# Norms between products in a two-layer trunk: one written order for all engines

## The chip, the cores and the metric

The kernel runs on one core of a Trainium2 chip. The metric is the device time in microseconds (us) from launch to the last store, as the median of several executions. One more execution was recorded by the hardware profiler; its trace gives start and length of each instruction on TensorE (PE, with its weight loads as PEld), VectorE (DVE), ScalarE (ACT), GpSimd (POOL) and SyncE (SP, which here only issues DMAs).

## The reference

Two layers over 512 tokens of 1024 features in float32. Each layer is a mixer and a gated MLP, and each of the two has a norm before and a norm after it:

```
x = x + rms_norm(mix, norm_gains[layer, 1])      # post-norm of the mixer
u = rms_norm(x, norm_gains[layer, 2])            # pre-norm of the MLP
ff = conv_ffn(u, ...)                            # 1024 -> 2 x 2816, conv of width 3, silu(gate) * val, -> 1024
x = x + rms_norm(ff, norm_gains[layer, 3])       # post-norm of the MLP
```

`rms_norm` divides each token's row by the root of its mean square (plus 1e-6) and multiplies by a gain per feature. The mixer of layer 0 runs four mLSTM heads and four gated DeltaNet heads, that of layer 1 eight HGRN2 heads; both end in a product with an output matrix of 1024 x 1024.

## The kernel before

**Precision.** Every large product is made of three matmuls on operands split in a high and a low part: high x high, high x low, low x high (`mm3`, lines 211 to 214). A weight piece of 128 x 1024 is loaded into a buffer `raw` (three of them), ACT copies the upper part (`whi`, line 230), and DVE or POOL subtracts it for the lower part (`wlo`, through the helper on line 101). `whi` and `wlo` have six places each, `PIECES`.

**Layout.** Tokens form four tiles of 128. The stream `xs` is kept with tokens in partitions. The normalised input `u` of a product is kept turned, features in partitions, as upper and lower parts `uh` and `ul` of eight blocks (k) by 512 tokens.

**A norm.** Of a post-norm, `postnorm_half` squares one half row of a product's PSUM bank on ACT (`token_square`, line 184, with the sum read out behind it) and multiplies the bank by the gain on DVE. `token_rsqrt` makes the root for 128 tokens: a sum on DVE (`tr_v`), Sqrt on ACT (`tk_y`), then a reciprocal and one Newton step on DVE (`tk_q`, `tk_r`). `postnorm_tile` adds bank times root to x, in two halves. The pre-norm `prenorm_tile` squares the halves of x, takes the root, scales to `un` (line 104), turns it by four PE transposes per half (`ut`, line 240), and ACT and DVE take the upper (line 235) and lower part into `uh` and `ul`.

**The three places.** `mix_out` multiplies the mixer's output with the output matrix: for column half n = 0, then n = 1, for all four token tiles t, 24 matmuls each into a bank `mo`; behind each (1, t) follows the post-norm of tile t, and behind some of them a pre-norm of one or two tiles, by the list `TAILS`. The MLP then starts with five pieces of the up-projection in two passes, first 256 tokens and last 256 (`EARLY`), so that PE can begin before the last tiles are normalised. The down-projection of the MLP keeps eight banks `dn` open; the last four of its 22 blocks are done bank by bank, and the norms follow in the same way, in layer 0 with the pre-norm of layer 1, whose first products are the value columns (`pt`), and in layer 1 with the stores.

**What sets the order.** Instructions written plainly are ordered per engine by a planner, by their place in the program and its own costs and readiness; a tile of a pool waits until its place is free. `then(f, ...)` ties an instruction behind the last one that was so tied on the same engine, so that these keep their written order on it; `now(f, ...)` issues plainly. A `tc.issue_after(ins)` block puts what it holds behind one instruction. All loads go through SP's queue in its order.

Of the kernel before, what the change touches and what calls it, by code (L numbers as in the profile page):

```python
# [18 lines left out]
P = 128  # L19
# [12 lines left out]
TAILS = ((0,), (1,), (), (2, 3))  # L32
# [3 lines left out]
def kernel(  # L36
# [24 lines left out]
    stop: int = 4,  # L61
# [65 lines left out]


# [10 lines left out]
    def load_x(xt, t, eng=nc.sync):  # L139
        eng.dma_start(out=xt[:, t, :], in_=x[0, t * P : (t + 1) * P, :])  # L140
# [42 lines left out]
    def now(f, **kw):  # L183
        f(**kw)

# [25 lines left out]
    def mm3(ps, lh, ll, rh, rl, start, stop):  # L211
        T.matmul(ps, lhsT=lh, rhs=rh, start=start, stop=False)  # L212
        T.matmul(ps, lhsT=lh, rhs=rl, start=False, stop=False)  # L213
        T.matmul(ps, lhsT=ll, rhs=rh, start=False, stop=stop)  # L214

    def load_w(src):
# [4 lines left out]
        nc.sync.dma_start(out=rv, in_=src)  # L221
        return rv
# [28 lines left out]
    def put_half(u, t, h, src):  # L251

        ps = mxt("ut")
        transpose4(ps, src, range(4))
        sl = (slice(None), slice(4 * h, 4 * h + 4), slice(t * P, (t + 1) * P))
        split_ps(u[0][sl], u[1][sl], v4(ps))

# [5 lines left out]
    def prenorm_tile(xt, t, g, u):  # L263
        ss = col(2, "ss")
        for h, hs in enumerate(halves):
            token_square(xt[:, hs], ss[:, h : h + 1])
        r = token_rsqrt(ss)
        for h, hs in enumerate(halves):
            un = half_t("un")
            stt(un, xt[:, hs], r, g[:, hs], ALU.mult, ALU.mult)  # L270
            put_half(u, t, h, un)

    def postnorm_half(ps, h, g, ss):

        token_square(ps, ss[:, h : h + 1])
        tt(V, ps, ps, g[:, halves[h]], ALU.mult)

    def postnorm_tile(xt, banks, ss):
        r = token_rsqrt(ss)
        for hs, ps in zip(halves, banks):  # L280
            stt(xt[:, hs], ps, r, xt[:, hs], ALU.mult, ALU.add)
# [55 lines left out]
    EARLY = ((0, 256), (256, 512))  # L337


    def ffn(layer, cw, cb, xs, tail):  # L340

        w_up, w_down = ffn_w_up[layer], ffn_w_down[layer]
        with tc.tile_pool(name=f"ffn{layer}", bufs=1) as fp:
            def t2(name, dt=F32, bufs=2, tag=None):
# [4 lines left out]
            yield lambda t: prenorm_tile(xs[t], t, gpre, u)  # L349
            gpost = gain(layer, 3)  # L350
            h0 = big["B"].tile([P, KD, S], F32, tag="h", name="h0")
            h2 = fp.tile([P, NF - 2 * KD, S], F32, tag="h2", name="h2")
            hT = [h0[:, f, :] for f in range(KD)] + [eighth(f, "h1") for f in range(KD)]
            hT += [h2[:, f, :] for f in range(NF - 2 * KD)]
            wc = [w_up[:, f * P : (f + 1) * P] for f in range(2 * NF)]
            early = feature_blocks(
                [piece(wc[i], V) for i in (0, NF, 1, NF + 1, 2)], u, EARLY, [bank(g, "pf") for g in ("pj", "pj", "sc", "po", "sc")]
            )
            for f in range(NF):
                pg = early.pop(0) if early else feature_block(wc[f], u)  # L360
# [4 lines left out]
                pv = early.pop(0) if early else feature_block(wc[NF + f], u)  # L365
# [4 lines left out]
            banks = [[bank(g, "dn") for g in tg] for tg in tags]  # L370
            dv = w_down.rearrange("(k p) c -> p k c", p=P)
            hs = {}
            last = 4

            def step(k, t, n):
# [3 lines left out]
                    banks[t][n], hi[:, tsl], lo[:, tsl], w[0][:, 0, halves[n]], w[1][:, 0, halves[n]], k == 0, k == NF - 1  # L379
                )  # L380

            for k in range(NF):
# [6 lines left out]
                if k < NF - last:  # L389
# [3 lines left out]
            for t in range(NT):  # L393
                ss = col(2, "ss2")
                for n in range(2):
                    for k in range(NF - last, NF):
                        step(k, t, n)
                    postnorm_half(banks[t][n], n, gpost, ss)
# [896 lines left out]
    for layer in range(2):  # L1295
# [31 lines left out]
        for _ in it:  # L1327
            pass
# [60 lines left out]
```

## Time and profile before

| | |
|---|---|
| median of 3 executions | 1344.22 us (1343.63 to 1344.73) |
| the profiled execution: time, and span of its instructions | 1344.86 us, 1343.1 us |
| PE busy | 1321.3 us, 98% of the span |
| DVE, ACT, POOL busy | 665.1, 613.5, 363.7 us |
| products of the up-projection and the like (`pf`), matmuls | 1168 on each of the lines 212, 213, 214 |
| granted TensorE clock, mean | 0.999 |

A row of the timeline holds the start, the length, engine, line, operation, the tile written and those read, the shape and the number of instructions merged, and in brackets the engine's idle time before it with what ended it. A row of a group holds, after the count, the busy time, the mean length in ns and the idle time before. Matmuls overlap, so their distance is read from start to start.

### The profile page before, as it was taken

The page shows a single profiled execution, that of the slowest core. Times are in us where ns is not written, and L with a number is a line of the kernel's source. Part 1 is how long each engine was busy: PE and PEld are TensorE (multiplying, and loading weights), DVE is VectorE, ACT ScalarE, POOL GpSimd, SP SyncE. Part 2 cuts the span into 40 slices and gives each one's busy share as a digit, 9 for nine tenths or more (in the row PEclk, how much of TensorE's full clock was granted, in tenths as well). Part 3 has the DMA queues.
Part 4 walks back from the last instruction along what each step waited for, and adds up shares of the span by engine and source line. Part 5 has one row for each costly group of instructions (what it writes and reads, how often), then busy time and mean ns, then how long its engine had stood idle before and what let it go on. Part 6 is the DMA issues. An engine that isn't in the chain of part 4 may idle for free.

```text
span 1343.1 us, 20271 instructions
## 1 busy us (share of the span) xinstructions
PE 1321.3 (98%) x8029; PEld 1096.8 (82%) x8029; DVE 665.1 (50%) x1321; ACT 613.5 (46%) x1158; POOL 363.7 (27%) x195
## 2 busy tenths in 40 slices
PE   8999999999999999999999999999999999999997
PEld 8787887888988888888878878877798888888886
DVE  6863774457543333311276784786756333332114
ACT  6754663545443333322356554564644333333222
POOL 1000000000665555544200000000036555554440
PEclk9999999999999999999999999999999999999999
DMA  6521131143333333222234123221323333322211
GB/s 176 163 64 37 48 95 50 43 157 99 95 110 94 94 101 103 95 95 94 94 94 113 64 61 94 69 74 32 106 83 111 98 104 97 95 94 94 97 61 63
DMA packets 165564, 121.25 MB, mean 90 GB/s; under 512 B 9246, under 2 KB 151006, under 8 KB 165470
## 3 DMA queue, kind: packets, MB, share of 16 engines
q1 hardware_dynamic: 165470, 119.96, 29.1%
q8 instruction: 63, 1.03, 0.3%
q14 instruction: 31, 0.25, 0.1%
HBM read 117.85 MB, written 2.10 MB: 89 GB/s over the span
## 4 chain that ended last, share of the span: by engine, by line
PE 76%; DVE 6%; ACT 1%; issue 1%; DVEq 0%; ACTq 0%
PE pf L212 15%; PE pf L213 15%; PE pf L214 15%; PE dn L212 6%; PE dn L213 6%; PE dn L214 6%; PE mo L212 2%; PE mo L214 1%; DVE wlo L101 1%; PE mo L213 1%; PE lev L1135 1%; DVE xt L104 1%; PE pt L214 1%; PE pt L213 1%; PE pt L212 1%; DVE un L104 1%
## 5 line engine op out<-in xcount | busy, mean ns | idle before, releaser
L101 POOL TENSOR_TENSOR wlo<-raw,whi 128x1024 fp32r<-128x1024 f32 x122 | 294.1, 2411 | 628.2 <-ACT whi L230 333.4
L212 PE MATMUL pf<-uh,whi 128*128 128x512 f32 (+1 forms) x1168 | 442.0, 379 | 0.0
L213 PE MATMUL pf<-ul,whi 128*128 128x512 f32 (+1 forms) x1168 | 441.5, 378 | 0.4 <-DVE ul L101 0.4
L214 PE MATMUL pf<-uh,wlo 128*128 128x512 f32 (+1 forms) x1168 | 440.7, 377 | 0.0
L230 ACT CAST whi<-raw 128x1024 fp32r<-128x1024 f32 x206 | 215.9, 1050 | 226.0 <-PE pf L213 204.7
L104 DVE SCALAR_TENSOR_TENSOR acc<-pf,fcw,acc 128x511 f32<-128x511 f32 (+1 forms) x176 | 131.4, 749 | 279.8 <-ACT acc L332 276.9
L212 PEld LDWEIGHTS pf<-uh,whi 128*128 128x128 f32 x1168 | 219.8, 188 | 40.0 <-ACT uh L235 0.5
L213 PEld LDWEIGHTS pf<-ul,whi 128*128 128x128 f32 x1168 | 220.0, 188 | 38.9 <-DVE ul L101 0.9
L214 PEld LDWEIGHTS pf<-uh,wlo 128*128 128x128 f32 x1168 | 220.0, 188 | 38.2
L212 PE MATMUL dn<-whi,hh 128*128 128x512 f32 x352 | 137.2, 390 | 0.0
L214 PE MATMUL dn<-whi,hl 128*128 128x512 f32 x352 | 137.0, 389 | 0.0
L213 PE MATMUL dn<-wlo,hh 128*128 128x512 f32 x352 | 137.0, 389 | 0.0
L101 DVE TENSOR_TENSOR wlo<-raw,whi 128x1024 fp32r<-128x1024 f32 x84 | 105.4, 1257 | 60.2 <-ACT whi L230 56.5
L101 DVE TENSOR_TENSOR hl<-h,hh 128x512 fp32r<-128x512 f32 x44 | 31.6, 717 | 160.4 <-ACT hh L386 160.3
L386 ACT CAST hh<-h 128x512 fp32r<-128x512 f32 x44 | 27.4, 623 | 152.3 <-PE dn L213 131.5
L212 PEld LDWEIGHTS dn<-whi,hh 128*128 128x128 f32 x352 | 66.1, 188 | 14.2 <-issue 0.5
L213 PEld LDWEIGHTS dn<-wlo,hh 128*128 128x128 f32 x352 | 66.1, 188 | 13.7
L214 PEld LDWEIGHTS dn<-whi,hl 128*128 128x128 f32 x352 | 66.1, 188 | 13.7
L753 POOL TENSOR_SCALAR_AFFINE_SELECT dec<-dec 128x512 f32<-128x512 f32 x8 | 7.3, 909 | 243.9 <-DVE dec L101 178.7
L332 ACT ACTIVATE acc<-pf,fcb,fcw 128x512 f32<-128x512 f32 x88 | 68.1, 774 | 8.2 <-POOL sg L101 5.7
L101 POOL TENSOR_TENSOR sg<-sg,acc 128x512 f32<-128x512 f32 x44 | 57.9, 1315 | 31.0 <-ACT sg L363 31.0
L363 ACT ACTIVATE sg<-acc 128x512 f32<-128x512 f32 x44 | 27.8, 632 | 67.0 <-DVE acc L104 67.0
(344 smaller groups left out, 1601.1 us busy)
## 6 DMA issues: line engine op xcount, KB each, us to landing
raw<-in_ffn_w_up_dram SPq DMA_DIRECT2D x88, 512.0 KB, 3.8
raw<-in_ffn_w_down_dram SPq DMA_DIRECT2D x44, 512.0 KB, 3.2
raw<-in_c_w_in_dram SPq DMA_DIRECT2D x32, 512.0 KB, 4.0
raw<-in_ab_w_in_dram SPq DMA_DIRECT2D x26, 512.0 KB, 3.7
gain<-in_norm_gains_dram SPq DMA_DIRECT2D x8, 512.0 KB, 5.2
raw<-in_ab_w_out_dram SPq DMA_DIRECT2D x8, 512.0 KB, 3.9
raw<-in_c_w_out_dram SPq DMA_DIRECT2D x8, 512.0 KB, 4.0
x<-in_x_dram SPq DMA_DIRECT2D x4, 512.0 KB, 5.9
```

The source lines that it names most:

```text
L101: return eng.tensor_tensor(out=o, in0=a, in1=b, op=op)
L104: return V.scalar_tensor_tensor(out=o, in0=a, scalar=s, in1=b, op0=op0, op1=op1, **kw)
L212: T.matmul(ps, lhsT=lh, rhs=rh, start=start, stop=False)
L213: T.matmul(ps, lhsT=lh, rhs=rl, start=False, stop=False)
L214: T.matmul(ps, lhsT=ll, rhs=rh, start=False, stop=stop)
L230: A.copy(out=hv, in_=rv)
L332: A.activation(out=acc, in_=ps, func=AF.Identity, scale=taps[:, K - 1 : K], bias=bias)
L363: A.activation(out=sg, in_=ag, func=AF.Sigmoid)
L386: A.copy(out=hi, in_=hT[k])
L753: G.affine_select(out=v4(d), in_=v4(d), pattern=[[0, NT], [1, P]], compare_op=ALU.is_ge, fill=-BIG, base=0, channel_multiplier=-1,)
L1135: T.matmul(pl4[i * 64 : (i + 1) * 64, c], lhsT=kr[:, c * P + i * 64 : c * P + (i + 1) * 64], rhs=qf[:, :, at : at + 32], start=True, stop= ...
```

## The change

`TAILS`, `prenorm_tile`, `postnorm_half` and `postnorm_tile` go. A class `Norms` holds the same steps as single functions, each issued through `then`; `root` issues the sum and the Sqrt at once and returns the rest, for the gain product to be put between. Three functions write out the order in which all engines go through the three kinds of norm:

- `mix_out` (both layers): the products of tiles 0 to 2 of half 0, then (1,0), (1,1), (1,2), (0,3), (1,3), then three early pieces. The second two weight pieces of half 1 are split into the places of `hh` and `hl`, two up pieces ahead of the norms into `w2` and `acc`, a third between them. x of tiles 2 and 3 is loaded behind the first two up pieces.
- `into_next` (from layer 0 to 1): the four pieces of value weights are split first, two into `w2` and `acc`; the four value products take the place of the first `token_blocks` of the mixer.
- `last_norm` (end): the order of before, with the first two steps of the root ahead of the gain product.

Three MLP pieces instead of five are done in halves; the other two are split behind the norms. In layer 1's mixer the three pieces of a head are fetched and split together at its start.

```
+    class Norms:
+        def root(self, t, second=False):
+            steps = []
+            self.roots[t] = token_rsqrt(self.ss[t][second], lambda f, **kw: steps.append((f, kw)))
+            for f, kw in steps[:2]:
+                then(f, **kw)
+            return lambda: [then(f, **kw) for f, kw in steps[2:]]
...
+    def mix_out(w_dram, order, yhi, ylo, gpost, xs, fetch, gpre, u, wc, t2, w2):
...
+                rv = load_w(wv[:, 2 * q : 2 * q + 2, halves[n]])
+                if n and i > 1:
+                    late.append((q, rv))
+                    continue
+                hi, lo = split_w(rv, V)
...
+        def products(n, t, ins=(), do=then):
+            b = banks[n, t] = bank((("pj", "pj", "pj", "pj"), ("sc", "sc", "po", "sc"))[n][t], f"mo{t}")
+            sl = slice(t * P, (t + 1) * P)
+            for i, k in enumerate(order8):
+                for f in dict(ins).get(i, ()):
+                    f()
+                mm3(b, yhi[:, k, sl], ylo[k][:, sl], *ws[n, k], i == 0, i == KD - 1, do)
...
+        for t in range(2):
+            fetch(t)
+        for t in range(3):
+            products(0, t, do=now)
+            nm.squares(0, t, now)
+            nm.gains(0, t, now)
+        for q, rv in late:
+            late_split(q, rv)
+        raws = [raw(i) for i in EARLY[:2]]
+        for t in (2, 3):
+            fetch(t, then)
+        split(raws[:1], spare[:1], spare[1:2])
...
+        products(1, 0)
+        nm.squares(1, 0)
+        rest = nm.root(0)
+        nm.gains(1, 0)
+        rest()
+        nm.residual(0, 0)
+        nm.squares2(0, 0)
...
+        rest = nm.root(2)
+        products(0, 3, ((5, [nm.turned(1, 0)]), (6, [nm.turned(1, 1)])))
+        r_ = raw(EARLY[2])
...
+        products(1, 3)
+        take(lambda k: hi2[:, k, :], lambda k: lo2[:, k, :], "sc")
+        early(0, 0, ((4, [nm.turned(2, 0)]), (7, [nm.turned(2, 1)])))
+        nm.squares(1, 3)
+        rest = nm.root(3)
+        nm.gains(1, 3)
+        nm.upper(2, 0)
+        rest()
+        nm.upper(2, 1)
+        nm.residual(3, 0)
+        nm.squares2(3, 0)
+        nm.lower(2, 0)
+        nm.residual(3, 1)
+        nm.squares2(3, 1)
+        nm.lower(2, 1)
+        rest = nm.root(3, True)
+        rest()
+        nm.scaled(3, 0)
+        nm.scaled(3, 1)
+        early(1, 0)
+        early(2, 0, ((3, [nm.turned(3, 0)]), (6, [nm.turned(3, 1)])))
+        for h in range(2):
+            nm.upper(3, h)
+            nm.lower(3, h)
+        for i in range(len(EARLY)):
+            early(i, S // 2)
...
+            with tc.issue_after(last[A].ins), tc.issue_after(last[V].ins):
+                more = [piece(wc[i], V) for i in (NF + 1, 2)]
...
+    def into_next(products, nm, wcols, spare):
...
+        for h in range(2):
+            nm.residual(3, h)
+            nm.squares2(3, h)
+        values(0)
+        values(1, ((2, [nm.turned(2, 0)]), (3, [nm.turned(2, 1)])))
+        for h in range(2):
+            nm.upper(2, h)
+            nm.lower(2, h)
+        rest = nm.root(3, True)
...
+    def last_norm(products, nm, store):
+        for t in range(NT):
+            for n in range(2):
+                products(t, n)
+                nm.squares(n, t)
+                if n:
+                    rest = nm.root(t)
+                nm.gains(n, t)
+            rest()
+            for h in range(2):
+                nm.residual(t, h)
+            store(t)
...
-            pf = feature_block(cols_of(1024, h), u, V)
+                pieces = [piece(cols_of(c, h), V) for c in (1024, 0, 3072)]
+            pf = feature_blocks(pieces[:1], u)[0]
```

More of the change, by code (lines that the diff above doesn't have):

```diff
@@ L261, with place @@
     halves = [slice(h * 512, (h + 1) * 512) for h in range(2)]
[L263 to L281, printed above, removed]
+    def place(u, t, h):
+        return (u[:, 4 * h : 4 * h + 4, t * P : (t + 1) * P])
     def piece(wcols, eng=None):
@@ L335, in conv, with __init__, squares, gains @@
         return acc
-    EARLY = ((0, 256), (256, 512))
-    def ffn(layer, cw, cb, xs, tail):
+    EARLY = (0, NF, 1)
+    class Norms:
+        def __init__(self, banks, gpost, xs, gpre=None, u=None):
+            self.banks, self.gpost, self.xs, self.gpre, self.u = banks, gpost, xs, gpre, u
+            self.ss = [[col(2, name) for name in ("ss2", "ss")] for _ in range(NT)]
+            self.roots, self.uns, self.uts = [None] * NT, {}, {}
+        def squares(self, n, t, do=then):
+            token_square(self.banks[n, t], self.ss[t][0][:, n : n + 1], do)
+        def gains(self, n, t, do=then):
+            b = self.banks[n, t]
+            do(V.tensor_tensor, out=b, in0=b, in1=self.gpost[:, halves[n]], op=ALU.mult)
+        def root(self, t, second=False):
[4 more added lines that the diff above has]
+            return lambda: [then(f, **kw) for f, kw in steps[2:]]
+        def residual(self, t, h):
+            x_ = self.xs[t][:, halves[h]]
+            then(
+                V.scalar_tensor_tensor, out=x_, in0=self.banks[h, t], scalar=self.roots[t], in1=x_,
+                op0=ALU.mult, op1=ALU.add,
+            )
+        def squares2(self, t, h):
+            token_square(self.xs[t][:, halves[h]], self.ss[t][1][:, h : h + 1], then)
+        def scaled(self, t, h):
+            hs = halves[h]
+            un = self.uns[t, h] = half_t("un")
+            then(
+                V.scalar_tensor_tensor, out=un, in0=self.xs[t][:, hs], scalar=self.roots[t], in1=self.gpre[:, hs],
+                op0=ALU.mult, op1=ALU.mult,
+            )
+        def turned(self, t, h):
+            def f():
+                ps = self.uts[t, h] = mxt("ut")
+                for j in range(4):
+                    sl = slice(j * P, (j + 1) * P)
+                    then(T.transpose, out=ps[:, sl], in_=self.uns[t, h][:, sl], identity=ident)
+            return f
+        def upper(self, t, h):
+            then(A.copy, out=place(self.u[0], t, h), in_=v4(self.uts[t, h]))
+        def lower(self, t, h):
+            hi, lo = (place(x_, t, h) for x_ in self.u)
+            then(V.tensor_tensor, out=lo, in0=v4(self.uts[t, h]), in1=hi.bitcast(F32), op=ALU.subtract)
@@ L342, in ffn @@
+    def ffn(layer, cw, cb, xs, fetch, w_out, order, yu, gpost, store):
         w_up, w_down = ffn_w_up[layer], ffn_w_down[layer]
@@ new lines, in products @@
+            def products(t, n, ins=()):
+                for i, k in enumerate(range(NF - ahead, NF)):
+                    for f in dict(ins).get(i, ()):
+                        f()
+                    step(k, t, n, then)
+            if layer == 0:
+                u = new_u()
+                w2 = h2("w2", F32R)
+                spare = [*(w2[:, i, :] for i in range(NF - 2 * KD)), *(t2("acc", F32R) for _ in range(2))]
+                pts = into_next(
+                    products, Norms(banks, gpost, xs, gain(1, 0), u), c_w_in[0][:, 2048:2560],
+                    spare,
+                )
+                return u, pts
```

310 lines of the change are left out of this document (222 added, 88 removed).

## The prediction

> **What bounds the kernel now.** I read first the page's busy times, then the busy times by stretches of 20 us, because a share over the whole span says nothing about the four places that the diff touches.
>
> ```profile
> PE 1321.3 (98%) x8029; PEld 1096.8 (82%) x8029; DVE 665.1 (50%) x1321; ACT 613.5 (46%) x1158; POOL 363.7 (27%) x195
> ...
> 300.00:320.00 20.00, 19.11 (x93) 15.29 (x92) 15.61 (x37) 13.23 (x30) 0.00 (x0) 1.00 0.23 67
> ...
> 680.00:700.00 20.00, 18.97 (x91) 14.77 (x90) 18.45 (x44) 13.89 (x40) 0.56 (x2) 1.00 0.43 129
> ...
> 960.00:980.00 20.00, 17.70 (x109) 15.01 (x109) 18.39 (x39) 12.56 (x28) 2.43 (x1) 1.00 0.41 125
> ```
>
> After the length, the columns are PE, PEld, DVE, ACT and POOL busy, the granted clock (1.00) and DMA. PE is the bound; DVE is nearly full just where PE has holes. These are the norms: after the mixer of layer 0, from layer 0's MLP into layer 1, after the mixer of layer 1. Busy time hides part of the loss, since matmuls overlap, so I read starts in PE's timeline (start, duration). First the norm after layer 0's mixer:
>
> ```profile
> 308.07 0.39 PE L214 MATMUL mo<-whi,ylo 128*128 128x512 f32 x1
> 308.30 0.60 PE L240 MATMUL ut<-ident,un 128*128 128x128 f32 x4
> 308.65 0.48 PE L212 MATMUL mo<-whi,yhi 128*128 128x512 f32 x1
> ...
> 316.48 0.39 PE L214 MATMUL mo<-whi,ylo 128*128 128x512 f32 x1
> 317.48 1.29 PE L240 MATMUL ut<-ident,un 128*128 128x128 f32 x8 [0.62 <-DVE un L104]
> 318.78 0.50 PE L212 MATMUL pf<-uh,whi 128*128 128x256 f32 x2
> 319.51 0.39 PE L213 MATMUL pf<-ul,whi 128*128 128x256 f32 x1 [0.22 <-DVE ul L101]
> ...
> 325.96 0.28 PE L213 MATMUL pf<-ul,whi 128*128 128x256 f32 x1
> 326.08 0.28 PE L214 MATMUL pf<-uh,wlo 128*128 128x256 f32 x1
> 327.13 0.63 PE L240 MATMUL ut<-ident,un 128*128 128x128 f32 x4 [0.77 <-DVE un L104]
> ```
>
> A full product takes 0.23 from start to start (308.07 to 308.30), one of 256 columns 0.12 (325.96 to 326.08), four transposes 0.35 (308.30 to 308.65). From 316.48 to 318.78 are 2.30 us for one product and eight transposes, worth 0.93: 1.37 lost. To 319.51, 0.73 for two half products: 0.49 lost. From 326.08 to 327.13: 0.93 lost. Together 2.8. The other two norms, in the same view:
>
> ```profile
> 695.83 0.39 PE L214 MATMUL pt<-whi,ul 128*128 128x512 f32 x1
> 696.72 1.29 PE L240 MATMUL ut<-ident,un 128*128 128x128 f32 x8 [0.51 <-DVE un L104]
> 698.03 0.50 PE L212 MATMUL pt<-whi,uh 128*128 128x512 f32 x1
> ...
> 699.21 0.66 PE L240 MATMUL ut<-ident,un 128*128 128x128 f32 x4 [0.45 <-DVE ul L101]
> ...
> 968.70 0.39 PE L214 MATMUL mo<-whi,ylo 128*128 128x512 f32 x1
> 971.02 0.50 PE L212 MATMUL pf<-uh,whi 128*128 128x256 f32 x2
> 971.74 0.39 PE L213 MATMUL pf<-ul,whi 128*128 128x256 f32 x1 [0.22 <-DVE ul L101]
> ...
> 978.31 0.28 PE L214 MATMUL pf<-uh,wlo 128*128 128x256 f32 x1
> 980.01 0.63 PE L240 MATMUL ut<-ident,un 128*128 128x128 f32 x4 [1.42 <-DVE un L104]
> ```
>
> Into layer 1: 2.20 for 0.93, and 1.18 for two products worth 0.46: 2.0 lost. After layer 1's mixer: 2.32 for 0.93, 0.72 for 0.24, 1.70 for 0.12: 3.45 lost. All three: **8.2 us**. By the idle times in brackets (0.62, 0.22, 0.77; 0.51, 0.45; 0.22, 1.42) it would be 4.2.
>
> The Trainium skill (Perfetto Trace Analysis, Identifying the Most-Contended Engine) says that matmul busy share is no good measure of distance to the roofline, since pipelined PE instructions look smaller in the trace. This trace agrees at the holes: by the bracketed idle times they are worth 4.2 us, by starts 8.2.
>
> Why DVE is late there stands in its own timeline:
>
> ```profile
> 314.17 1.23 DVE L101 TENSOR_TENSOR wlo<-raw,whi 128x1024 fp32r<-128x1024 f32 x1
> 315.31 0.15 DVE L184 SCALAR_TENSOR_TENSOR tk_r<-tk_q,tk_y 128x1 f32<-128x1 f32 x1
> ...
> 316.59 1.41 DVE L104 SCALAR_TENSOR_TENSOR un<-xt,tk_r,gain 128x512 f32<-128x512 f32 x2
> ```
>
> A weight split of the coming MLP (1.23) stands before the last step of a norm's root, and a second one fills most of 315.31 to 316.59; without the two, un could start some 2.4 us sooner, more than the hole before it is long.
>
> **The change part by part.** *Order and splits.* All engines get one written order in the three norms. The first splits of the next stage go ahead of the norms into free places (w2, acc, hh, hl), and the last token tile's products of half 0 move behind tile 2's of half 1. Beside the halves below, products, transposes, norm instructions and weight DMAs keep their count. What the norms cost per tile:
>
> ```profile
> L104 DVE SCALAR_TENSOR_TENSOR un<-xt,tk_r,gain 128x512 f32<-128x512 f32 x8 | 5.7, 748 | 0.1
> L101 DVE TENSOR_TENSOR ul<-ut,uh 128x512 fp32r<-128x512 f32 x8 | 5.4, 690 | 1.4 <-ACT uh L235 1.4
> L184 ACT ACTIVATE junk<-xt 128x512 bf16<-128x512 f32 x8 | 5.1, 631 | 3.7 <-DVE xt L104 2.1 <-issue 1.5
> L235 ACT CAST uh<-ut 128x512 fp32r<-128x512 f32 x8 | 4.7, 586 | 6.6 <-PE ut L240 6.3
> ```
>
> On DVE two gains (0.70 each), two residuals and two scalings (0.75), two lower parts (0.69) and eight small steps (about 0.2): 7.4 us. PE needs 24 x 0.23 + 8 transposes = 6.2 per group of products. DVE is the slower by 1.2, and four tiles take 30 us. PE's cover: after the mixers, from (1,0)'s end, four groups (25 us) and the first halves (10), 35 us; into layer 1, from (0,0)'s end, 19 us of down products and 18 of values, 37 us. So it fits, but with some 5 us over a whole norm, and single places can be late.
>
> The tightest is tile 3 after the mixers. From the end of products (1,3): square 0.8, first root step 0.2, gain 0.7 (the Sqrt beside it), three small steps 0.55; residual at 2.4 to 3.15, then lower(2,0) ahead of the second residual, done at 4.5; square 0.85, root 1.2, scaling: 7.35. Its transposes stand after 24 + 24 + 9 half products and two groups of transposes: 57 x 0.12 + 0.7 = 7.5. Level; I allow 0.3 per mixer. Its last lower part comes at about 10.0, the second halves begin at 72 x 0.12 + 1.4 = 10.0 and need that part 12 products later: covered. Tile 1's transposes stand 15 products (3.4) into (0,3), its scaling ends 3.5 to 3.6 after (1,2): 0.2 per mixer. So 0.5 stays at each mixer. Into layer 1 I add the rows in the written order. The eight splits (0.7 each on DVE) end about 2 us after (0,0)'s products, as the places of weight pieces come free only then. Tile 0's transposes then come 0.1 late, tile 1's 0.4. Tile 2's upper and lower parts stand behind both residuals and squares of tile 3, 0.5 late: 1.0 stays. Kept 2.0 of 8.2: **gain 6.2**. Bounds: 8.2 if nothing is late; nothing if each moved wait ends where the old one did.
>
> *Queues.* Squares of (1,0) now stand on ACT behind two up-piece copies, and those behind their loads on SP. x of tiles 2 and 3 is loaded behind these two, and x waits for the mixer's memory anyway:
>
> ```profile
> 284.21 0.75 DVE L104 SCALAR_TENSOR_TENSOR y<-yt,cmix,gs 128x512 f32<-128x512 f32 x1
> ...
> 285.04 2.85 SPq L140 DMA_DIRECT2D xt<-in_x_dram  x4
> ```
>
> The four go out as the last mixer read ends (284.96). From there the last head's upper and lower part (0.6 and 0.7 by the rows above) end near 286.3, the nine products that need them near 288.4, (1,0) near 294. Tile 0's x is wanted 3 us later, 12 after its issue. The second up piece can load only when a late split has freed its buffer, about 289:
>
> ```profile
> raw<-in_ffn_w_up_dram SPq DMA_DIRECT2D x88, 512.0 KB, 3.8
> ```
>
> At 3.8 us, or 5 beside x, it lands as (1,0) ends. If later, squares, gains and all behind them wait, but tile 0's transposes have about 1 us to spare: cost 0, bounds 0 and 2. The gain row of layer 1 and the four value weights go out before the norms and stay covered by 20 us of down products.
>
> *Mixer ends.* PE fills the wait for the last head with products of half 0: before four tiles, now three. It already lacks a little:
>
> ```profile
> 936.39 0.39 PE L213 MATMUL mo<-wlo,yhi 128*128 128x512 f32 x1
> 937.15 0.33 PE L240 MATMUL yt<-ident,yn 128*128 128x128 f32 x1 [0.37 <-DVE yn L101]
> ```
>
> In layer 1 three tiles hold 3 x 7 x 3 = 63 products that need no last head; 59 have run with the row of 936.39 (counted in PE's timeline from 917 on), the other four end near 938.4, and the last lower part comes near 939.9 (937.15 + 0.35, then y, upper and lower at 0.7, 0.6, 0.7): up to 1.5 open, less where products of half 1 slip in. I take 0.3 for both layers, between 0 and 2.
>
> *Halves.* Three instead of five MLP pieces are done in halves: a piece takes 48 x 0.12 = 5.76, whole 24 x 0.23 = 5.52. Four pieces over two layers: **gain 1.0**. The last two of the five are split only after the norms, 18 us of PE work after (1,3), so they're there in time.
>
> *Last norm.* The first root step moves ahead of the gain product:
>
> ```profile
> 1336.99 0.70 DVE L101 TENSOR_TENSOR dn<-dn,gain 128x512 f32<-128x512 f32 x1 [1.69 <-ACT junk L184]
> 1337.60 0.20 DVE L184 TENSOR_SCALAR tr_v<-ss 128x1 f32<-128x1 f32 x1
> ...
> 1338.07 0.17 DVE L184 RECIPROCAL tk_y<-tk_y 128x1 f32<-128x1 f32 x1 [0.27 <-ACT tk_y L184]
> ```
>
> The Sqrt then runs under the gain: reciprocal at 1336.99 + 0.12 + 0.61 = 1337.72 and not 1338.07, **gain 0.35**, all on the path to the end.
>
> *Layer 1's pieces* are fetched three at a time per head. ACT and DVE have room, PE is full there: 0, bounds 1 either way.
>
> **Sum.** 6.2 + 1.0 + 0.35 - 0.3 = 7.3. The profiled execution took 1344.86 with a span of 1343.1; 1337.6 by it. It lies 0.6 above the median 1344.22, so 1336.9 for the median.
>
> **The rivals.** *All is covered*: 8.2 + 1.0 + 0.35 = 9.6, and smaller holes that I didn't quote add up to 0.7: 1334.1. For it: 5 us of cover per norm. Against it: level places and DVE slower per tile than PE.
>
> *POOL in the chain.* Only the first splits are tied to the written order; those of the third pair of MLP pieces go to POOL and may start inside tile 3's chain. What that does:
>
> ```profile
> 320.42 2.41 POOL L101 TENSOR_TENSOR wlo<-raw,whi 128x1024 fp32r<-128x1024 f32 x1 [54.04 <-ACT whi L230]
> ...
> 321.62 2.30 DVE L101 TENSOR_TENSOR wlo<-raw,whi 128x1024 fp32r<-128x1024 f32 x1
> ```
>
> The DVE split, 1.23 alone, ended 1.09 after POOL's end at 322.83. A scaling reads two SBUF operands too; caught so, tile 3 is up to 2.2 later in each mixer norm: 4.4 less, 1341.3. Against it: POOL's pieces wait for buffers and for loads behind two others. The Trainium skill (SBUF — State Buffer, Who interferes with whom) says that a VectorE instruction with two SBUF inputs and a GpSimd one that reads SBUF block each other wholly; the trace agrees, 2.30 us with the end 1.09 after POOL's.
>
> *The order is stuck on a load*: squares of (1,0) wait for a late up piece, or tile-wise lateness adds up in the in-order engines, and the new waits equal the old 8.2. Only 1.0 + 0.35 - 0.3 is left: 1343.2.
>
> *Slower: the early splits starve the last head.* Place: DVE at each mixer's end, where a dozen 0.2 us steps of the last head's root precede yn. Four late halves and two up pieces (4 x 0.7 + 1.23 + 1.4 = 5.4 us) slip between them, as the split at 314.17 did, and PE has three tiles of filler. Each mixer end then opens by up to 5.4, 10.8 in all: 1347.7. It decides from 7.3 on, two thirds of the splits inside the chain. Against it: x could be written only when the mixer's memory was given back (284.96), and the places for the splits lie in a pool opened then, behind the root.
>
> **How the numbers follow.** Forecast 0.54 (1335 to 1339), all covered 0.18, POOL 0.12, stuck 0.09, starved 0.07. The range 1333.5 to 1341.6 leaves out the last two and a little more. A measurement of this kernel tells 0.2%, 2.7 us, from no change. Faster holds the first three: 0.84; same, most of stuck: 0.08; slower 0.08.
>
> **What would show it.** Right: around the three norms no un or ul wait on PE over 0.5; no weight split inside a root; the transposes in twos and fours between products; 144 half products per layer (three pieces) in place of 240; the reciprocal of the last tile about 0.35 sooner after its square. Wrong: PE idle before yt or mo at 284 and 938, ACT's squares waiting for a copy of raw, a POOL split beside a scaling.

## The result, and the profile after

The changed kernel takes **1336.62 us** (median of 4, 1334.82 to 1337.07) against 1343.97 us of the kernel before on the same chip (median of 4): ratio 0.9942, interval 0.9925 to 0.9959. A second timing, beside an experiment below, gave 1335.77 against 1344.98, ratio 0.9929 (0.9916 to 0.9943): about 0.6% faster. The profiled execution took 1337.02 us with a span of 1334.2.

The forecast was 1336.9. The spans say more than the times: 1343.15 before, 1334.18 after, **8.97 us less**, where the sum had 7.3. The first profiled execution after has 2.8 us outside its span, that of before and the second one after have 1.7, so the forecast hit the first median a little by luck.

PE's busy share is up by a point; the 96 matmuls fewer are the halves (in each layer 96 half products became 48 whole ones).

```profile
PE 1316.5 (99%) x7933; PEld 1091.4 (82%) x7933; DVE 664.3 (50%) x1331; ACT 612.6 (46%) x1168; POOL 364.4 (27%) x195
```

By stretches of 20 us (length; PE, PEld, DVE, ACT, POOL busy; granted clock; DMA), PE is full in all three norms:

```profile
300.00:320.00 20.00, 20.00 (x108) 16.91 (x107) 16.80 (x41) 9.68 (x28) 0.00 (x0) 1.00 0.09 28
...
680.00:700.00 20.00, 20.00 (x100) 16.57 (x99) 13.25 (x31) 10.24 (x32) 0.00 (x0) 1.00 0.15 54
960.00:980.00 20.00, 20.00 (x149) 19.00 (x147) 15.69 (x34) 10.33 (x23) 1.03 (x1) 1.00 0.20 61
```

PE's timeline at the places where the prediction showed holes: half products at their 0.12, transposes in fours between them, no bracket. From the last product to the first half product are 0.23 us where 2.30 and eight transposes lay before.

```profile
317.38 0.39 PE L124 MATMUL mo<-hh,ylo 128*128 128x512 f32 x1
317.61 0.28 PE L124 MATMUL pf<-uh,w 128*128 128x256 f32 x1
317.72 0.28 PE L124 MATMUL pf<-ul,w 128*128 128x256 f32 x1
...
325.18 0.28 PE L124 MATMUL pf<-uh,wlo 128*128 128x256 f32 x1
325.30 0.60 PE L124 MATMUL ut<-ident,un 128*128 128x128 f32 x4
...
721.39 0.69 PE L1417 MATMUL lev<-q,k 128*64 128x64 f32 x16
722.93 0.88 PE L1445 MATMUL lev<-qf,k 128*64 128x96 f32 x16 [0.86 <-DVE qf L99]
```

The last two rows are new: head 0 of layer 1's mixer now waits. DVE's timeline has the first half of the set-apart tile's scaling done 0.24 us before its transposes (324.31 + 0.75 = 325.06, against 325.30):

```profile
311.01 1.23 DVE L124 TENSOR_TENSOR wlo<-raw,whi 128x1024 fp32r<-128x1024 f32 x1 [1.21 <-ACT whi L124]
312.15 0.16 DVE L124 RECIPROCAL tk_y<-tk_y 128x1 f32<-128x1 f32 x1
...
324.31 1.41 DVE L124 SCALAR_TENSOR_TENSOR un<-xt,tk_r,gain 128x512 f32<-128x512 f32 x2
...
1328.39 0.21 DVE L124 TENSOR_SCALAR tr_v<-ss 128x1 f32<-128x1 f32 x1 [2.02 <-ACT junk L124]
1328.52 0.69 DVE L124 TENSOR_TENSOR dn<-dn,gain 128x512 f32<-128x512 f32 x1
1329.12 0.15 DVE L124 RECIPROCAL tk_y<-tk_y 128x1 f32<-128x1 f32 x1
```

Since effects of 1 us are near what a time can tell, I compare stretches between first rows of a kind in PE's timeline: A from layer 0's first mixer-output product (`mo`) to its first down product (`dn`), B from there to layer 1's first level product (`lev`), C to layer 1's first `mo`, D to its first `dn`. Each experiment is one execution and one profile, but for the last two, which were timed several times. Where no edit touches a stretch, B and D repeat within 0.1 us from run to run, A within 0.1 or 0.4 (its transposes of tile 1 stand so close that some runs wait there); C scatters from 191.3 to 192.2.

| us | A | B | C (heads) | D | span |
|---|---|---|---|---|---|
| before | 300.35 | 163.68 | 190.18 | 299.00 | 1343.15 |
| changed | 296.69 | 161.72 | 191.56 | 294.68 | 1334.18 |
| changed, again | 296.67 | 161.76 | 191.68 | 294.69 | 1334.06 |
| splits in the root, DVE | 303.77 | 161.75 | 191.27 | 301.94 | 1348.21 |
| the same, POOL | 306.40 | 161.70 | 191.33 | 303.23 | 1352.41 |
| one split in the root | 298.70 | 161.74 | 191.39 | 298.23 | 1338.66 |
| four tiles per half | 303.21 | 161.77 | 191.61 | 300.08 | 1347.23 |
| the same, split moved | 300.17 | 161.79 | 191.63 | 298.27 | 1341.88 |
| ACT, DVE by the planner | 301.63 | 162.78 | 190.49 | 301.79 | 1345.39 |
| five pieces in halves | 297.73 | 161.78 | 192.15 | 295.33 | 1336.55 |
| head 1 behind `f` | 296.74 | 161.78 | 191.78 | 294.68 | 1335.01 |
| head 0 untied | 296.77 | 166.75 | 190.48 | 294.69 | 1337.12 |
| two pieces in gaps | 296.67 | 161.77 | 190.41 | 294.70 | 1333.25 |

Change against before: A -3.66, B -1.96, C **+1.38**, D -4.32, the rest -0.4, of which the last norm has 0.36. Neither profile has a step at a halved clock before its very end, so these differences are PE's waits and products alone.

### The profile page after: what moved, and what is told of

Read it like the earlier page. It is cut to its first block, busy times and chain, and to the rows that moved or that the text cites. A ratio compares the mean times of both kernels' runs of the same rounds, so it can differ in the third digit from the quotient of the medians.

```text
span 1334.2 us, 20085 instructions
## 1 busy us (share of the span) xinstructions
PE 1316.5 (99%) x7933; PEld 1091.4 (82%) x7933; DVE 664.3 (50%) x1331; ACT 612.6 (46%) x1168; POOL 364.4 (27%) x195
## 4 chain that ended last, share of the span: by engine, by line
PE 79%; DVE 3%; ACT 1%; DMA 1%; issue 0%; DVEq 0%; ACTq 0%
PE pf L127 43%; PE dn L127 15%; PE mo L124 4%; PE dn L124 3%; PE pf L124 3%; PE mo L127 2%; PE pt L127 2%; PE lev L1445 1%; PE pt L124 1%; PE ut L124 1%; DVE wlo L99 1%; DMA raw<-in_c_w_in_dram 1%; PE o L1484 1%; DVE qk L99 0%; PE yt L238 0%
## 5 line engine op out<-in xcount | busy, mean ns | idle before, releaser
L127 PE MATMUL pf<-uh,whi 128*128 128x512 f32 x1040 | 409.2, 393 | 0.0
L127 PE MATMUL pf<-ul,whi 128*128 128x512 f32 x1040 | 408.6, 393 | 0.0
L127 PE MATMUL pf<-uh,wlo 128*128 128x512 f32 x1040 | 407.7, 392 | 0.0
L127 PEld LDWEIGHTS pf<-uh,whi 128*128 128x128 f32 x1040 | 195.3, 188 | 40.5 <-issue 0.2
L127 PEld LDWEIGHTS pf<-uh,wlo 128*128 128x128 f32 x1040 | 195.4, 188 | 40.1
L127 PEld LDWEIGHTS pf<-ul,whi 128*128 128x128 f32 x1040 | 195.3, 188 | 39.2
L127 PE MATMUL dn<-whi,hh 128*128 128x512 f32 x288 | 112.2, 390 | 0.0
L127 PE MATMUL dn<-whi,hl 128*128 128x512 f32 x288 | 112.0, 389 | 0.0
L127 PE MATMUL dn<-wlo,hh 128*128 128x512 f32 x288 | 112.0, 389 | 0.0
L99 DVE TENSOR_TENSOR wlo<-raw,whi 128x1024 fp32r<-128x1024 f32 x70 | 85.3, 1223 | 44.8 <-ACT whi L228 41.4
```

The source lines that it names most:

```text
L99: return eng.tensor_tensor(out=o, in0=a, in1=b, op=op)
```

## The experiments

Each is an edit of the changed kernel; all compute the whole result.

**Two splits inside the root of the tile set apart.** Ahead of its pre-norm root:

```
+        for r_ in [raw(i) for i in (NF + 1, 2)]:
...
+            then(A.copy, out=hl[0], in_=r_)
+            then(V.tensor_tensor, out=hl[1], in0=r_, in1=hl[0].bitcast(F32), op=ALU.subtract)
         rest = nm.root(3, True)
```

> In both mixers' norms the two up pieces that are split only after the norms are split in the middle of the token tile that is set apart, between the second half of its square sum and its root, the lower part on DVE. Theory (a weight split inside a norm's root was what made PE wait): two splits of 1.23 us push that tile's scaling back by about 2.4 us, its transposes are wanted 0.24 us after the scaling, so PE waits about 2.2 us on the scaled tile at each mixer, and the stretch from a mixer's output products to its down products is longer by about 2.2 us twice, 4.4 in all. Rival (the holes came from the norms' own length on DVE or from the order of the transposes, the splits only stood beside them): PE's wait stays under 0.5 us at each place and the two stretches stay within 0.3 us of the changed kernel's 296.69 and 294.68.

The theory holds, but its price was far too small: A and D grew by 7.1 and 7.3, 14.3 in all instead of 4.4. DVE's timeline, then POOL's, then PE's:

```profile
324.17 2.36 DVE L124 TENSOR_TENSOR wlo<-raw,whi 128x1024 fp32r<-128x1024 f32 x2 [1.19 <-ACT whi L124]
...
327.13 1.62 DVE L124 SCALAR_TENSOR_TENSOR tk_q<-tk_y,tr_v 128x1 f32<-128x1 f32 x1
...
328.98 1.42 DVE L124 SCALAR_TENSOR_TENSOR un<-xt,tk_r,gain 128x512 f32<-128x512 f32 x2
```

```profile
326.12 2.61 POOL L99 TENSOR_TENSOR wlo<-raw,whi 128x1024 fp32r<-128x1024 f32 x1 [59.83 <-ACT whi L228]
```

```profile
329.88 1.09 PE L124 MATMUL ut<-ident,un 128*128 128x128 f32 x4 [4.37 <-DVE un L124]
...
330.97 0.41 PE L124 MATMUL pf<-ul,whi 128*128 128x256 f32 x1
331.19 0.41 PE L124 MATMUL pf<-uh,wlo 128*128 128x256 f32 x1
```

The scaling is 4.6 us later than without the edit: 0.94 for ACT's copy, 2.28 for the two splits, and 1.40 because `tk_q`, a step of 0.22 us on 128 numbers, took 1.62 and ended with POOL's split (326.12 + 2.61). That split is a later piece's and began at 330.96 in the changed kernel, so the edit brought it forward too. Less the 0.24 of slack, PE waits 4.37. The rest of the 7.1 lies behind the wait: half products start every 0.21 us, not 0.12, for some 5 us. A window of this run shows why; the granted clock (third from the end), 1.00 up to the wait, is halved:

```profile
332.00:335.00 3.00, 3.00 (x16) 3.00 (x15) 0.92 (x2) 1.23 (x2) 0.76 (x1) 0.50 0.83 251
```

**The same with the lower parts on POOL** (`V.tensor_tensor` becomes `G.tensor_tensor`), so that DVE gets no instruction more.

> As the run with two splits inside the set-apart tile's root, but the lower parts are computed on POOL, so DVE has no instruction more. Theory of the locked engines (a DVE instruction with two SBUF inputs does not end while a POOL instruction on SBUF runs, as 2.30 us instead of 1.23 in the kernel before): the scaling of that tile is held until about 0.6 us after POOL's first or second split has ended, PE waits 1 to 4 us on the scaled tile at each mixer, and the two stretches grow by 2 to 8 us together. Rival (only DVE's own queue counts): PE's wait stays under 0.5 us and the two stretches stay within 0.3 us of 296.69 and 294.68.

A and D grew by 9.7 and 8.6, PE waited 6.38 and 6.42 us. The first timeline is DVE's, the second POOL's:

```profile
326.03 1.20 DVE L124 SCALAR_TENSOR_TENSOR tk_q<-tk_y,tr_v 128x1 f32<-128x1 f32 x1
327.26 2.26 DVE L124 SCALAR_TENSOR_TENSOR tk_r<-tk_q,tk_y 128x1 f32<-128x1 f32 x1
329.56 3.46 DVE L124 SCALAR_TENSOR_TENSOR un<-xt,tk_r,gain 128x512 f32<-128x512 f32 x2
```

```profile
324.83 4.67 POOL L124 TENSOR_TENSOR wlo<-raw,whi 128x1024 fp32r<-128x1024 f32 x2 [58.24 <-ACT whi L124]
329.47 2.33 POOL L99 TENSOR_TENSOR wlo<-raw,whi 128x1024 fp32r<-128x1024 f32 x1
```

Three DVE steps in a row, 0.22, 0.16 and 0.75 us long by themselves, each last until a POOL split has ended (the first ends 327.23; the second 329.52, POOL's pair 329.50). That is 5.1 us of lateness; the other 1.5 is the Sqrt, which stood behind the two copies on ACT. Queue order on DVE can't explain it: that POOL's splits hold these steps up is shown. The Trainium skill (SBUF — State Buffer, Who interferes with whom) has a DVE instruction with two SBUF inputs contend with a GpSimd one that reads SBUF; this run agrees, and shows that the DVE instruction may be as small as 128x1. The prediction priced this rival at 2.2 us per mixer, one split's length; here three steps in a row were caught, the third by the POOL split of the next piece (329.47).

**One split only in the root**, the other left behind the norms.

> As the run with two splits on DVE inside the set-apart tile's root, with one only; the other stays behind the norms. In the run with two, PE waited 4.4 us at each mixer (1.2 for ACT's copy, 2.4 for the splits, 1.4 for a small DVE step that ended with a POOL split, less the slack) and then started half products every 0.21 us instead of 0.12 for some 5 us, 2.6 us more. Theory: one split less takes 1.2 us or, if the POOL split then also misses the chain, 2.6 us from the wait, so PE waits 1.6 to 3.2 us at each mixer. If the slower starts come after any long wait, they show again in proportion (1 to 2 us more per mixer); if they come only past a length of wait between 1.4 us (the kernel before, where the starts stayed at 0.12) and 4.4 us, a wait under that length shows none, and the stretch grows by the wait alone.

PE waited 1.82 and 1.83 us. DVE's split began 1.35 after its last step and the root 1.14 later; no POOL split was caught. Yet A grew by 2.0 and D by 3.6, because only the second wait was followed by slow starts. PE's timeline at both places:

```profile
326.33 0.63 PE L124 MATMUL ut<-ident,un 128*128 128x128 f32 x4 [1.82 <-DVE un L124]
...
327.40 0.28 PE L124 MATMUL pf<-uh,wlo 128*128 128x256 f32 x1
327.52 0.28 PE L124 MATMUL pf<-uh,whi 128*128 128x256 f32 x1
...
976.15 0.63 PE L124 MATMUL ut<-ident,un 128*128 128x128 f32 x4 [1.83 <-DVE un L124]
...
977.30 0.41 PE L124 MATMUL pf<-uh,wlo 128*128 128x256 f32 x1
977.52 0.41 PE L124 MATMUL pf<-uh,whi 128*128 128x256 f32 x1
```

So neither "in proportion" nor "past a length" describes it: two waits of one length differ. The last section has what sets them apart.

**The last tile not set apart.** Four tiles of half 0, then four of half 1:

```
-        for t in range(3):
+        for t in range(4):
...
-        products(0, 3, ((5, [nm.turned(1, 0)]), (6, [nm.turned(1, 1)])))
+        products(1, 3, ((5, [nm.turned(1, 0)]), (6, [nm.turned(1, 1)])))
```

> The last token tile is not set apart: after both mixers all four tiles' products of half 0 come first and then the four of half 1, so its norm starts only after the very last products; splits and written order stay. Theory (the set-apart tile gives its norm six products' groups of cover): the last tile's scaling comes about as late after its products as before (7.3 us by the rows of its steps), while only 24 + 9 half products, 4 us, and two groups of transposes stand between, so PE waits 2 to 3.5 us on the scaled last tile at each mixer and each of the two stretches grows by as much. Rival (the splits were all that stood in the way, DVE without them is quick enough): PE's wait stays under 0.5 us and the stretches within 0.3 us of 296.69 and 294.68.

A grew by 6.5, D by 5.4, but not as the theory had it. PE waited 1.6 to 1.7 us on tile 1's lower part and 1.9 on tile 2's scaled half, with slow starts behind the second. And DVE had a weight split between tile 2's Sqrt and its reciprocal. The changed kernel has it at the same place (311.01 above, 2.1 us between the Sqrt's end and the reciprocal) and loses nothing by it. So this run couldn't tell the cover from the split, and I moved the split behind tile 2's scaling:

> As the run with four tiles per half, but the third early piece is split after tile 2's scaling instead of inside tile 2's first root, where it took 2.1 us between the Sqrt and the reciprocal (the changed kernel has it at that place too). That run had two waits at each mixer: 1.6 to 1.7 us on tile 1's lower part and 1.9 us on tile 2's scaled half. Theory (the order without a tile set apart is itself too tight): the first wait goes, but the scaled half, 2.1 us sooner, still comes 1.6 us after its transposes are wanted (12 half products, 1.44 us, behind the last product), so PE waits 1.4 to 1.8 us at each mixer, and each of the two stretches is 1.5 to 3.5 us longer than 296.69 and 294.68, by whether half the clock follows. Rival (the split inside the root did it all): no wait over 0.5 us, and the stretches stay within 0.3 us.

The first wait went, the second stayed at 1.71 and 1.87 us, and one that I had not foreseen came up, 1.36 us twice on tile 3's scaling, which the split now precedes. A and D are 3.5 and 3.6 over the changed kernel, with no slow starts. Together that is 7.1 of the 8.0 us that A and D had won. The wait on tile 2, 1.71 and 1.87, is what the missing cover costs; the 1.36 on tile 3 comes with the split's new place (1.22 long) and isn't the cover's alone. So setting the tile apart is needed beside the early splits, but its own share of the 3.5 was not separated.

**ACT and DVE by the planner.** In the class of the norms' steps `then` becomes `now`; PE's order and the early splits stay. One thing more moves with it: the late splits are tied behind the last instruction that was so tied on ACT and DVE, and that is now an early split and no longer a norm's last step.

```
-        def squares(self, n, t, do=then):
+        def squares(self, n, t, do=now):
...
-                then(f, **kw)
-            return lambda: [then(f, **kw) for f, kw in steps[2:]]
+                now(f, **kw)
+            return lambda: [now(f, **kw) for f, kw in steps[2:]]
```

> The norms' steps on ACT and DVE are no longer held to a written order in the three norms; a planner puts them in again by its own costs, while PE keeps the written order of products and transposes, and the splits stay ahead of the norms in their places. Theory (what made the holes was the splits in the roots, and these are gone either way): PE's waits on scaled tiles and lower parts stay under 0.5 us at each place and the two stretches within 0.3 us of 296.69 and 294.68. Rival (the order of ACT and DVE is what saves the time): later splits slip into the roots again or tiles overtake each other, and 0.5 to 2 us come back at each mixer, 1 to 4 in all, and up to 2 into layer 1.

The rival holds, and at more than its price: A +4.9, B +1.1, D +7.1; the kernel is as slow as the one before. ACT's timeline shows a copy of a later piece, itself late by its load, in front of tile 2's square:

```profile
316.35 1.05 ACT L228 CAST whi<-raw 128x1024 fp32r<-128x1024 f32 x1 [0.64 <-DMA raw<-in_ffn_w_up_dram]
317.31 0.62 ACT L127 ACTIVATE junk<-xt 128x512 bf16<-128x512 f32 x1
```

PE waits 2.72 us there. In layer 1 it waits 4.98, some 2.1 of it since the scaling on DVE meets a POOL split that started 0.04 us before it (its first half took 2.84 instead of 0.75, the row holds both halves):

```profile
973.62 3.51 DVE L127 SCALAR_TENSOR_TENSOR un<-xt,tk_r,gain 128x512 f32<-128x512 f32 x2
```

```profile
973.58 2.34 POOL L99 TENSOR_TENSOR wlo<-raw,whi 128x1024 fp32r<-128x1024 f32 x1 [0.68 <-ACT whi L228]
```

Heads took 190.49: four splits begin inside the norm into layer 1, from 685.22 to 693.38, and B pays for it, as below. In the first mixer norm a late split stands in tile 2's root (310.14 on DVE). So the run shows what later splits cost that slip into the norms; how much of it the order of the norm's own steps would cost, with the late splits still tied, was not tested.

**Five pieces in halves**, as before the change.

```
-                return done.pop(i) if i in done else feature_blocks([more.pop(0) if more else piece(wc[i])], u)[0]
+                return done.pop(i) if i in done else feature_blocks([more.pop(0)], u, ((0, S // 2), (S // 2, S)))[0] if more else feature_block(wc[i], u)
```

> The two pieces that the change made whole again are done in halves as before the change, five pieces per layer instead of three; all else stays. Theory (a piece in halves costs PE 48 starts of 0.12 us against 24 of 0.23): 0.24 to 0.25 us for each of four pieces, so each of the two stretches from a mixer's output products to the down products grows by 0.5 us, 1.0 in all. Rival (halves cost nothing, since the PE's columns are the same and only the records differ): both stretches stay within 0.1 us of 296.69 and 294.68.

From the first half product on, both layers are 0.63 longer (242.69 against 242.06 and 242.05), 0.315 per piece instead of the expected 0.25. D shows it alone (+0.65); A has 0.4 more from before it, which the edit doesn't touch: the transposes of tile 1 waited 0.18 us at 309.59, as they did, 0.24, in the run with POOL in the root.

**Where head 0 loses.** The change ties head 0's three splits behind the norm. ACT's timeline of the changed kernel has a copy that waited for its load in front of head 0's table and `k`:

```profile
711.56 1.05 ACT L228 CAST whi<-raw 128x1024 fp32r<-128x1024 f32 x1 [1.00 <-DMA raw<-in_c_w_in_dram]
712.63 1.28 ACT L1522 ACT_TABLE_LOAD   x1
713.92 0.60 ACT L1522 ACTIVATE k<-pf 128x512 f32<-128x512 f32 x1
```

My first theory took that for the cause, so head 1's splits were tied behind head 0's last gate activation (`f`):

```
+                elif h == 1:
+                    st.enter_context(tc.issue_after(shaped.ins))
...
+            shaped = A.activation(out=f, in_=f, func=AF.Identity, scale=olb[:, h : h + 1], bias=lb[:, h : h + 1])
```

> In layer 1's mixer the splits of head 1's pieces are tied on ACT behind head 0's last gate activation; nothing else is moved. Theory (head 0 lost 1.26 us because an upper-part copy on ACT that waited for its load stood in front of head 0's table and k activations): the wait of 0.86 us before head 0's first level products is gone, head 0 takes 23.9 us again instead of 25.1, and layer 1's heads take 190.3 instead of 191.56. Rival (the three raw buffers are held by splits tied behind the norms, so the loads themselves are late and head 0's pieces or head 1's come too late in any order): the wait stays, or returns at head 1, and the heads take 191.3 or more.

`k` came at 711.19, 5.6 us after head 0's first product (705.55) instead of 8.9, and nothing was won: heads 191.78, PE waits 1.06 on the next `qf`. The theory fell: a late `k` is not the whole of it. DVE's timeline of this run has three splits in the head's own chain instead (the second at 715.83):

```profile
714.59 1.23 DVE L99 TENSOR_TENSOR wlo<-raw,whi 128x1024 fp32r<-128x1024 f32 x1
...
718.20 1.23 DVE L99 TENSOR_TENSOR wlo<-raw,whi 128x1024 fp32r<-128x1024 f32 x1
```

So I formed another: the tie moves three splits, and the loads behind them, out of the norm into head 0, and wherever they go there, they or the copies that wait for those loads cut into its chain (in the run above a copy of this kind ended at 721.55 in front of `qf`). First the tie was taken away:

```
-            with ExitStack() as st:
-                if not h:
-                    st.enter_context(tc.issue_after(last[A].ins))
-                    st.enter_context(tc.issue_after(last[V].ins))
-                pieces = [piece(cols_of(c, h), V) for c in (1024, 0, 3072)]
+            pieces = [piece(cols_of(c, h), V) for c in (1024, 0, 3072)]
```

> Only the tie of head 0's three pieces behind the norm into layer 1 is taken away: the planner puts their upper copies among that norm's steps again, and four more loads go out before the gain rows. Theory (head 0 is late by 1.26 us because the tie moved three splits of 1.23 us, and the loads behind them, from the norm into head 0's own DVE and ACT work): layer 1's heads take 190.2 to 190.5 instead of 191.56, and the price comes back in the norm into layer 1, where PE waits 0.5 to 2 us in all on scaled tiles or lower parts. If PE doesn't wait there, the whole 1.3 us is a gain. Rival (head 0 is late for another reason, such as a table load or the planner's order of the levels): the heads still take 191.3 or more.

Heads 190.48, the loss is gone; but the norm pays 5.0, more than I expected. DVE's timeline has three splits threaded into the root of tile 2's post-norm (the third at 681.31) and one more in that of its pre-norm (687.81), and PE waits 3.25 us (690.49) with slow starts after it:

```profile
678.84 1.23 DVE L99 TENSOR_TENSOR wlo<-raw,whi 128x1024 fp32r<-128x1024 f32 x1
679.98 0.21 DVE L124 SCALAR_TENSOR_TENSOR tk_q<-tk_y,tr_v 128x1 f32<-128x1 f32 x1
680.11 1.22 DVE L99 TENSOR_TENSOR wlo<-raw,whi 128x1024 fp32r<-128x1024 f32 x1
681.25 0.15 DVE L124 SCALAR_TENSOR_TENSOR tk_r<-tk_q,tk_y 128x1 f32<-128x1 f32 x1
```

Then two of the three were put at written places where ACT and DVE stood idle, one behind the last tile's scaling, one between its two lower parts:

```
         for h in range(2):
             nm.scaled(3, h)
+        split_early(1024)
         values(2, ((4, [nm.turned(3, 0)]), (6, [nm.turned(3, 1)])))
         for h in range(2):
             nm.upper(3, h)
             nm.lower(3, h)
+            if not h:
+                split_early(0)
```

`split_early` loads the piece and issues its copy and its subtraction through `then`.

> The changed kernel with two of head 0's three pieces split at written places inside the norm into layer 1, one after the last tile's scaling and one between its two lower parts, where ACT and DVE were idle for 2.4 and 1.9 us, and 0.7 and 1.1 us (their rows from 694 to 699 us of the changed kernel); the third stays behind the norm, and all else is in the same order. Theory (head 0 is late by what the tie moved into it, and the places of those splits decide what they cost): PE waits nowhere over 0.3 us in the norm into layer 1, its 40.06 us up to head 0's first level products stay within 0.2, and layer 1's heads take 190.4 to 190.8 instead of 191.56, so the time falls by 0.8 to 1.2 us against the changed kernel. Rival (the loads and not the splits make head 0 late): the heads take 191.3 or more. Second rival (the split in the gap meets the transposes after all): PE waits 0.5 us or more on the last tile's upper or lower part.

As the theory had it: B 161.77, heads 190.41, no wait of PE in the norm, and the wait in head 0 gone. DVE's timeline:

```profile
695.28 1.22 DVE L124 TENSOR_TENSOR wlo<-raw,whi 128x1024 fp32r<-128x1024 f32 x1
697.31 0.69 DVE L124 TENSOR_TENSOR ul<-ut,uh 128x512 fp32r<-128x512 f32 x1 [0.81 <-ACT uh L124]
698.27 1.23 DVE L124 TENSOR_TENSOR wlo<-raw,whi 128x1024 fp32r<-128x1024 f32 x1 [0.27 <-ACT whi L124]
```

On ACT the copy in front of head 0's table now waits for PE and no longer for its load, and `k` is back at 7.78 us after head 0's first product (705.17), as in the kernel before (718.39 after 710.61):

```profile
710.59 1.05 ACT L228 CAST whi<-raw 128x1024 fp32r<-128x1024 f32 x1 [2.42 <-PE pf L127]
...
712.95 0.60 ACT L1532 ACTIVATE k<-pf 128x512 f32<-128x512 f32 x1
```

It takes **1334.78 us** (4 runs, 1334.05 to 1334.97), ratio to the kernel before 0.9921 (0.9908 to 0.9935). The changed kernel was timed beside it:

> The changed kernel as it is, timed on the same chip as the run with two pieces split in the gaps. Every theory: 0.994 of the kernel before, with the stretches of its first profile within 0.4 us.

1335.77 (5 runs, 1335.14 to 1336.30). The runs of the two, timed side by side, don't overlap (in the first timing, on another chip, the changed kernel had one run of 1334.82); the version with two pieces in the gaps beats both kernels, the changed one by 1.0 us. Earlier splits also let later loads go earlier. In the changed kernel it was a load that the copy in front of `k` waited for, so these rows point to the loads; no run moves loads and splits apart, so the shares of the 1.3 us in the heads stay open.

## Why the prediction was right, and where it was wrong

Its result was right, by errors that cancel. The terms against what the stretches show:

| term of the sum | forecast | measured |
|---|---|---|
| holes at the three norms | 8.2 by rows, 2.0 of it kept | 8.7, nothing kept |
| halves | 1.0 | 1.26 |
| last norm | 0.35 | 0.36 |
| mixer ends | -0.3 | 0 |
| layer 1's pieces | 0 (bounds 1 either way) | -1.38 |
| sum | 7.3 | 9.0 of the span |

- **The holes by starts.** The cause was tried at the mixers: splits put back into a root bring waits back. For the norm into layer 1 it rests on the two runs in which later splits slipped in (B +1.1 and +5.0). A and D less the halves (0.63 each) give 3.03 and 3.69, B 1.96: 8.7, against 2.8, 3.45 and 2.0 counted from the rows. The 0.4 more is inside the 0.7 left for holes not quoted. The idle brackets (4.2) would have missed half of it.
- **The 2.0 that was to stay** is the step that failed first. I set level places against each other and let 0.3 and 0.2 stay at each mixer and 1.0 into layer 1; PE waits at none in this profile. Tile 1's 0.2 is nearest to right: 0.18 and 0.24 in two other runs of the same order, none in the rest. Tile 3's scaling is 0.24 us ahead of its transposes, where I had it level, and in the norm into layer 1 the first transposes follow their products at 0.23 (the two rows below, PE's timeline of the changed kernel). So of the rivals "all is covered" came true at the norms.

```profile
670.40 0.39 PE L124 MATMUL dn<-whi,hl 128*128 128x512 f32 x1
670.63 0.62 PE L124 MATMUL ut<-ident,un 128*128 128x128 f32 x4
```

- **Layer 1's pieces at 0, bounds 1 either way**, is the step that failed outright: -1.38. I costed the fetch in threes; what cost was the tie of head 0's splits behind the norm, which the change part named only as a fetch. Built with the fetches one at a time again, and the tie kept, the changed kernel has the same order on every engine, so the fetch is not the cause. "ACT and DVE have room" stood there without a row, and it is true: in the 16.42 us from head 0's first product to its first level DVE is busy 9.60 us and ACT 10.19 (before 8.92 and 9.07), with five splits begun on DVE (706.16 to 718.53) where there were three. What failed is the step from room to no cost: ACT idles 1.00 us on a copy's load right in front of what the head waits for.
- **Halves**: the mechanism was right, the term too small. A whole product starts every 0.227 us (316.02 to 317.38 is six of them), which I had rounded to 0.23: 48 x 0.12 - 24 x 0.227 = 0.31, not 0.24.
- **Mixer ends**: PE's gaps before the last head's transposes are the same as before (0.09 and 0.36 us, against 0.11 and 0.37); three products of half 1 slipped in at layer 1, as the prediction allowed.
- **Last norm**: the reciprocal comes 1.46 us after the square's start and not 1.80, as worked out.
- **The signs.** No wait on `un` or `ul`, transposes in fours and 144 half products were right. "No weight split inside a root" is wrong as a sign: tile 2's root has one at 311.01, and it costs nothing while the tile set apart gives PE other work. What counts is the lateness against that work.
- **The other rivals.** The squares of (1,0) did wait for an up piece's load, 3.00 us of idle ACT, and ran as (1,0) ended, at no cost: as worked out. The late halves were split from 285.50 on, behind the last head's upper part (284.97), so nothing starved. The first POOL split came at 330.96, behind tile 3's chain; its price would have been 1.4 us of lateness (one step caught, as with the splits on DVE) to 5.1 (three, as with the splits on POOL), where I gave it 2.2.

## What to carry to other kernels

Where one engine is full, ask of each helper instruction how late it may be against the work that stands in front of its consumer, and write the order out where that margin is shorter than what could slip in front (0.24 us here, against splits of 1.23): a planner that goes by readiness puts weight copies in front of norm steps, and with the norms' order and the ties of the late splits left to it the span was 11 us longer here. Work moved out of a tight place needs a place of its own: the splits tied behind the norm cost head 0 1.4 us, and 1.0 us of the time came back by naming two gaps for them. And read busy shares in the stretch where the moved work lands, not over the whole.

## What the runs showed of the hardware that I had not expected

**A wait of PE can cost up to about twice its length, and whether it does is partly chance.** Behind a wait the granted clock fell to 0.50, and half products started every 0.21 us instead of 0.12; in the run with one split in the root 1.83 us of wait so lengthened D by 3.6. The traces say when. In all thirteen profiles every change of the granted clock lies a whole number of steps of 3.413 us behind the first one (to 0.002 us), and a halved stretch within the kernel is one, two or three steps long. What follows a step at the full clock goes by how long PE was idle in it: up to 1.73 us the full clock stayed, from 2.03 us on it was always halved. Of the four steps between, those with 1.83, 1.84 and 1.85 us were followed by half the clock, one with 1.87 was not.

So a wait matters by how it falls on the steps. In the run with one split in the root, the wait of 1.82 us is cut by the border at 325.14 into 0.63 and 1.19; the one of 1.83 lies wholly in one step. Those two steps each, in windows:

```profile
321.73:325.14 3.41, 2.78 (x24) 2.58 (x22) 1.76 (x5) 1.61 (x4) 0.00 (x0) 1.00 0.01 2
325.14:328.55 3.41, 2.22 (x20) 2.25 (x20) 2.33 (x5) 0.63 (x2) 0.00 (x0) 1.00 0.66 201
973.67:977.08 3.41, 1.58 (x14) 1.41 (x13) 2.62 (x7) 0.47 (x2) 0.00 (x0) 1.00 0.43 124
977.08:980.49 3.41, 3.41 (x18) 3.41 (x17) 1.32 (x2) 1.56 (x3) 0.00 (x0) 0.50 0.10 30
```

The two waits of 1.71 and 1.87 us of the run with the split moved are cut by a border too, and the 1.42 of the kernel before lies in one step but is too short. The first change comes 4.1 to 7.3 us after the first instruction, another place in each run, so the prices of waits near 1.8 us above are one draw each.

The Trainium skill (TensorE: Matmul & The Clock Gate, What's actually happening) has the clock halved after an idle window of about 3.4 us that runs freely, without regard to when work starts. The freely running window agrees with these runs; that all of it must be idle doesn't, since 1.83 us of 3.41 were enough here.

**POOL holds up even the smallest DVE steps.** Steps on 128 numbers took 1.62, 1.20 and 2.26 us beside a weight split on POOL, and 0.16 to 0.22 alone. In a chain of small steps each one can be caught anew.
